# Wider modulation products through one row buffer, a softmax division and GpSimd's work on other engines, and a half-spectrum Fourier branch in both layers

## The chip, the cores and the metric

The kernel runs on one core of a Trainium2 chip. Its engines are TensorE (PE; its weight loads are PEld), VectorE (DVE), ScalarE (ACT), GpSimd (POOL), and SyncE (SP), which issues the DMAs; each runs its own instructions in order. The metric is the device time in microseconds of one execution.

## The reference

Two layers of a diffusion backbone, over 256 latent tokens (x) and 256 context tokens (ctx), 2048 channels wide. Both streams go through the same weights, each with its own modulation vector:

```python
mod = silu(c) @ ada_w[l] + ada_b[l]          # 3 x 2048: shift, scale, gate; once for c, once for c_ctx
h = rmsnorm(x, norm_g[l]) * (1 + scale) + shift
q, k, v, u_pool, u_four, g = split(h @ w_in[l])   # 1024, 256, 256, 512, 512, 2048
att  = attention(rope(norm(q)), rope(norm(k)), v)  # 8 heads, 2 kv heads; latents see context + latents
pool = multiscale_pool(u_pool, pool_w, pool_scale)
four = real(fft2(u_four per group of 128 channels, ortho)) @ fourier_w
x = x + gate * ((concat(att, pool, four) * silu(g)) @ w_out[l])
```

The second layer computes the latents alone past k and v, and the output is `rmsnorm(x, final_norm_g)` of the latents. The words "layer 1" and "layer 2" below mean the first and the second; in the code they are l = 0 and l = 1.

## The kernel before

**Matmuls.** All activations are held transposed (channels on the partitions), tokens as columns: 512 of them in layer 1, 256 of the latents in layer 2 past k and v. Each product of two fp32 matrices is made of three matmuls of fp32r halves (hi x hi, lo x hi, hi x lo; `mm3`, L331 to L333). A weight piece of 512 KB comes through `wpiece`: a DMA into `raw` (L146), ScalarE's cast to `whi` (L139), VectorE's subtraction to `wlo` (L140). Each of these three has 3 buffers. A piece is good for 24 matmuls 512 wide, or 48 narrower ones.

**The order of the work.** The program is written as one stream: in each layer the chunks of the input projection (pooling channels, Fourier channels, k and v, then two of q), with the branches' steps fed in between (`side`), then the gate tiles (`gate_evac`: tanh on ScalarE, `th`), the split of the gated mixed activations into `mh` and `ml`, and the output projection of 16 tiles (`finish`: `x` plus gate times the product at L676, its square `sq`, and the running sum of squares `accv`). A scheduler turns it once into a fixed list for each engine, by data dependences, buffers and priorities. Evacuations and weight pieces run at a higher priority (AHEAD), the modulation products at a low one (LOW).

**The modulation products.** Layer 1's shift and scale are made at the start by TensorE. The rest, gate of layer 1 and all of layer 2, is made by VectorE: 64 units of 128 rows of ada_w, transposed in `adar`, each times `cbt`, silu(c) and silu(c_ctx) on all partitions, with the sum over the row taken by the same instruction (`accum_out`, L189). Units below 48 need two products, for c and c_ctx, the last 16 one. A row of 2048 elements is done in two halves of 1024, in separate visits: 128 half units, 224 products. The buffers are

```python
cbt = rp.tile([P, 2, 1024], F32, tag="cbt", bufs=1, ...)
raw = rp.tile([P, 1024], F32, tag="araw", ...)          # rp has bufs=2
junk = rp.tile([P, 1024], BF16, tag="ajunk", bufs=1, ...)  # the products themselves, never read
```

`fill(n)` takes n steps of this generator after each weight piece (the fractions in FILL), and `fill_to` takes what is still due: 32 steps (16 units) ahead of layer 1's output projection, 96 at `between`, which stands in that projection's last tile and makes layer 2's scale and shift (`ab_98`, `ada_cols`) and its first `xn`, and 128 in layer 2. Each load waits by hand for the split of the weight piece that was last written (`pace`).

**The other places.** `rsqrt_small` (six calls, the q and k norms) starts on VectorE and runs three Newton steps of four operations on GpSimd. In the attention a head's probabilities `p` come from ScalarE's exp with their sum in `nm`, and VectorE multiplies by its reciprocal (L550); TensorE then transposes them (L562). `finish` adds the squares on GpSimd (L686, L688). The Fourier branch does two stages of matmuls: over the positions with a table (`dh`, `dl`), and over the channels with the folded tables `fh`, `fl`. Layer 1 uses the half table `dft0` (256 columns, cosines and sines of half of the spectrum) and restores the other half by a sum and a difference (`second0`); layer 2 uses the full one, `dft`, of 512 columns (`second1`).

The names `t2`, `f4`, `q8` are pools of general buffers: `t2` has 11 of 2 KB a partition, for `th`, `sq`, `p`, `xn`, `kraw` and the like.

## Time and profile before

| what | us |
| --- | --- |
| median of 3 runs | 1109.19 (1108.81 to 1110.93) |
| span of the profiled execution (its only time on the page) | 1107.6 |
| PE busy | 1066.2 |
| DVE busy | 849.3 |
| ACT busy | 451.7 |
| POOL busy | 83.0 |
| modulation products (L189), busy | 283.6 |

The span runs from the first to the last instruction of the profiled execution; the times of the runs hold what lies around it too. Busy shares are shares of the span. A group's row gives the line, the engine, the operation, output <- inputs, partitions x elements and the count; then busy time in us and the mean of one in ns; then the idle time of that engine just ahead of them, and what ended it. In the chain, a share is time in which the end of the program waited for this engine.

### The profile page before, as it was taken

The page shows a single profiled execution, that of the slowest core. Times are in us where ns is not written, and L with a number is a line of the kernel's source. Part 1 is how long each engine was busy: PE and PEld are TensorE (multiplying, and loading weights), DVE is VectorE, ACT ScalarE, POOL GpSimd, SP SyncE. Part 2 cuts the span into 40 slices and gives each one's busy share as a digit, 9 for nine tenths or more (in the row PEclk, how much of TensorE's full clock was granted, in tenths as well). Part 3 has the DMA queues.
Part 4 walks back from the last instruction along what each step waited for, and adds up shares of the span by engine and source line. Part 5 has one row for each costly group of instructions (what it writes and reads, how often), then busy time and mean ns, then how long its engine had stood idle before and what let it go on. Part 6 is the DMA issues. An engine that isn't in the chain of part 4 may idle for free.

```text
span 1107.6 us, 15377 instructions
## 1 busy us (share of the span) xinstructions
PE 1066.2 (96%) x5724; PEld 881.1 (80%) x5724; DVE 849.3 (77%) x1513; ACT 451.7 (41%) x741; POOL 83.0 (7%) x106
## 2 busy tenths in 40 slices
PE   5999999999899999999999999899999999999995
PEld 3566677888688888888888777788887899999995
DVE  6358647996968789999969998889646989767554
ACT  5223224323314554432522123288325656446552
POOL 0000000002003001000001111100002210001220
PEclk9899999999899999999999999999999999999998
DMA  9999667466653243566876777655665555765553
GB/s 358 406 334 336 226 230 242 158 192 198 214 185 118 73 143 124 153 205 232 283 249 220 225 220 257 208 170 177 239 192 171 166 190 170 260 206 187 184 180 94
DMA packets 66603, 231.89 MB, mean 209 GB/s; under 512 B 7200, under 2 KB 12384, under 8 KB 62944
## 3 DMA queue, kind: packets, MB, share of 16 engines
q1 hardware_dynamic: 66528, 230.91, 62.4%
q8 instruction: 45, 0.74, 0.3%
q14 instruction: 30, 0.25, 0.1%
HBM read 228.77 MB, written 2.11 MB: 208 GB/s over the span
## 4 chain that ended last, share of the span: by engine, by line
PE 74%; DVE 11%; DMA 8%; issue 4%; ACT 2%; POOL 1%; SPq 0%; DVEq 0%; ACTq 0%
PE mm L333 17%; PE mm L331 17%; PE mm L332 17%; PE mm L829 7%; DMA araw<-in_adar 5%; DVE ajunk L189 5%; PE sm L829 4%; DVE wlo L140 3%; PE sm L892 2%; PE sm L332 2%; PE sm L331 2%; PE sm L333 2%; PE sm L562 1%; DMA x<-in_xT 1%; ACT whi L139 1%
## 5 line engine op out<-in xcount | busy, mean ns | idle before, releaser
L140 DVE TENSOR_TENSOR wlo<-raw,whi 128x1024 fp32r<-128x1024 f32 (+1 forms) x216 | 256.1, 1186 | 125.0 <-ACT whi L139 124.4
L139 ACT CAST whi<-raw 128x1024 fp32r<-128x1024 f32 (+1 forms) x216 | 219.1, 1018 | 299.7 <-PE mm L332 134.3
L189 DVE SCALAR_TENSOR_TENSOR ajunk<-araw,cbt 128x1024 bf16<-128x1024 f32 x224 | 283.6, 1266 | 60.7 <-DMA araw<-in_adar 42.2
L333 PE MATMUL mm<-mh,wlo 128*128 128x256 f32 (+1 forms) x528 | 176.3, 334 | 6.2 <-DVE wlo L140 6.0
L331 PE MATMUL mm<-mh,whi 128*128 128x256 f32 (+1 forms) x528 | 175.1, 332 | 0.0
L332 PE MATMUL mm<-ml,whi 128*128 128x256 f32 (+1 forms) x528 | 174.8, 331 | 0.0
L331 PE MATMUL mm<-whi,hh 128*128 128x512 f32 x416 | 168.6, 405 | 4.5 <-DVE gpart L635 3.5
L332 PE MATMUL mm<-wlo,hh 128*128 128x512 f32 x416 | 164.3, 395 | 1.1 <-DVE wlo L140 1.1
L333 PE MATMUL mm<-whi,hl 128*128 128x512 f32 x416 | 164.0, 394 | 0.0
L331 PE MATMUL mm<-hh,whi 128*128 128x256 f32 (+1 forms) x452 | 151.0, 334 | 0.0
L332 PE MATMUL mm<-hl,whi 128*128 128x256 f32 (+1 forms) x452 | 149.1, 330 | 0.0
L333 PE MATMUL mm<-hh,wlo 128*128 128x256 f32 (+1 forms) x452 | 149.1, 330 | 0.0
L333 PEld LDWEIGHTS mm<-mh,wlo 128*128 128x128 f32 x528 | 100.2, 190 | 20.7 <-DVE wlo L140 11.6
L332 PEld LDWEIGHTS mm<-ml,whi 128*128 128x128 f32 x528 | 100.2, 190 | 9.7
L331 PEld LDWEIGHTS mm<-mh,whi 128*128 128x128 f32 x528 | 100.2, 190 | 9.3 <-ACT whi L139 0.4
L331 PEld LDWEIGHTS mm<-whi,hh 128*128 128x128 f32 x416 | 78.9, 190 | 21.9 <-DVE gpart L635 3.9
L332 PEld LDWEIGHTS mm<-wlo,hh 128*128 128x128 f32 x416 | 79.0, 190 | 17.6 <-DVE wlo L140 1.9
L333 PEld LDWEIGHTS mm<-whi,hl 128*128 128x128 f32 x416 | 78.8, 189 | 17.6 <-DVE hl L140 0.3
L333 PEld LDWEIGHTS mm<-hh,wlo 128*128 128x128 f32 x452 | 85.7, 190 | 8.2
L332 PEld LDWEIGHTS mm<-hl,whi 128*128 128x128 f32 x452 | 85.7, 190 | 7.9
L331 PEld LDWEIGHTS mm<-hh,whi 128*128 128x128 f32 x452 | 85.7, 190 | 7.6
L679 ACT ACTIVATE sq<-x 128x256 f32<-128x256 f32 (+1 forms) x33 | 16.9, 513 | 114.1 <-DVE x L676 114.1
(197 smaller groups left out, 1372.1 us busy)
## 6 DMA issues: line engine op xcount, KB each, us to landing
araw<-in_adar SPq DMA_DIRECT2D x128, 512.0 KB, 4.1
raw<-in_wb SPq DMA_DIRECT2D x78, 512.0 KB, 3.9
raw<-in_wo SPq DMA_DIRECT2D x64, 512.0 KB, 3.7
raw<-in_wg SPq DMA_DIRECT2D x55, 512.0 KB, 4.2
a<-in_ada SPq DMA_DIRECT2D x24, 1024.0 KB, 7.7
a<-in_ada SPq DMA_DIRECT2D x16, 512.0 KB, 5.0
x<-in_xT SPq DMA_DIRECT2D x4, 1024.0 KB, 7.2
cbt<-cd SPq DMA_DIRECT2D x7, 512.0 KB, 5.8
```

The source lines that it names most:

```text
L139: i = S.copy(hi, src)
L140: V.tensor_sub(lo, src, hi.bitcast(F32))
L189: V.scalar_tensor_tensor(junk, raw, 1.0, cbt[:, v], op0=ALU.mult, op1=ALU.mult, accum_out=acc[:, u, h, v : v + 1])
L331: PE.matmul(o, ah, bh, start=start, stop=False)
L332: PE.matmul(o, ah, bl, start=False, stop=False)
L333: PE.matmul(o, al, bh, start=False, stop=stop)
L562: PE.transpose(tp[:, h * P : h * P + P], ps[h][:, i * P : i * P + P], idt)
L679: S.activation(sq, x, AF.Square)
L829: PE.matmul(o, lt, r, start=s0, stop=s1)
L892: PE.matmul(a[32 * g : 32 * g + 32, :w_], cs[:, k], raw[:, i], start=kk == k_first, stop=kk == npc - 1, tile_position=(0, 32 * g))
```

## The change

Modulation products: a unit is one visit, 2048 wide, 112 products in all. `rp` has one buffer: one `cbt` of [128, 2, 2048] for the whole kernel, loaded once, and one `araw` of 2048, filled by two DMAs of 512 KB (L175). The first product of a unit below 48 writes its products as 8-bit floats into a tile of `t2` (L183, `ajunk`); a unit's last product writes them back into `araw` itself. A unit is still two steps of `fill`, the first of them after its first load. The sums of the two halves (`tensor_reduce`) are gone.

The softmax division goes from VectorE to ScalarE (L532). The additions of squares go from GpSimd to VectorE (L668); the first square is written into `accv` directly. A Newton step is three operations on VectorE instead of four on GpSimd. The Fourier branch uses `dft0` and `second` (the former `second0`, with `nst` streams) in both layers: layer 2's first stage has 24 matmuls of 256 columns instead of 512, the second 24 of 130 and 128 instead of 256. The `f4` pool has 4 buffers instead of 5.

```diff
-    late = {"f4": ctx.enter_context(tc.tile_pool(name="f4p", bufs=5))}
+    late = {"f4": ctx.enter_context(tc.tile_pool(name="f4p", bufs=4))}
...
-    acc = const.tile([P, 64, 2, 2], F32, name="acc")
+    acc = const.tile([P, 64, 2], F32, name="acc")
...
     def ada_units():
         rp = late["rp"]
-        cbt = None
-        segs = (
-            [(u, 0) for u in range(16)],
-            [(u, 1) for u in range(48)],
-            [(u, 0) for u in range(16, 64)],
-            [(u, 1) for u in range(48, 64)],
-        )
-        for seg in segs:
-            h = seg[0][1]
+        with tc.high_priority(offset=LOW):
+            cbt = rp.tile([P, 2, D], F32, tag="cbt", name="cbt")
+            for v in range(2):
+                nc.sync.dma_start(cbt[:, v], late["cd"][v].partition_broadcast(P))
+        for u in range(64):
             with tc.high_priority(offset=LOW):
-                cbt = rp.tile([P, 2, 1024], F32, tag="cbt", bufs=1, name=name("cbt"))
-                for v in range(2 if seg[0][0] < 48 else 1):
-                    nc.sync.dma_start(cbt[:, v], late["cd"][v, 1024 * h : 1024 * h + 1024].partition_broadcast(P))
-            for u, _ in seg:
-                with tc.high_priority(offset=LOW):
-                    raw = rp.tile([P, 1024], F32, tag="araw", name=name("araw"))
-                    d = nc.sync.dma_start(raw, adar[u, h])
+                raw = rp.tile([P, D], F32, tag="araw", name=name("araw"))
+                for h in range(2):
+                    c = slice(1024 * h, 1024 * h + 1024)
+                    d = nc.sync.dma_start(raw[:, c], adar[u, h])
                     tc.add_manual_dep(
                         d.ins, pace[0].ins.name, mybir.DependencyInfo(mybir.DependencyClass.Sync, mybir.DependencyReason.DATA)
                     )
-                    for v in range(2 if u < 48 else 1):
-                        junk = rp.tile([P, 1024], BF16, tag="ajunk", bufs=1, name=name("ajunk"))
-                        V.scalar_tensor_tensor(
-                            junk, raw, 1.0, cbt[:, v], op0=ALU.mult, op1=ALU.mult, accum_out=acc[:, u, h, v : v + 1]
-                        )
-                yield u
+                    if h == 0:
+                        yield u
+                for v in range(2 if u < 48 else 1):
+                    junk = t2("ajunk", (P, D), F8) if u < 48 and v == 0 else raw
+                    V.scalar_tensor_tensor(
+                        junk, raw, 1.0, cbt[:, v], op0=ALU.mult, op1=ALU.mult, accum_out=acc[:, u, v : v + 1], saturate=False
+                    )
+            yield u
...
     def ada_cols(dst, u0, b0):
         n = KT
-        V.tensor_reduce(dst, acc[:, u0 : u0 + n].rearrange("p u h v -> p u v h"), axis=AX.X, op=ALU.add)
-        V.tensor_add(dst, dst, adab[:, b0 : b0 + n].unsqueeze(2).to_broadcast([P, n, 2]))
+        V.tensor_add(dst, acc[:, u0 : u0 + n], adab[:, b0 : b0 + n].unsqueeze(2).to_broadcast([P, n, 2]))
...
-            G.tensor_mul(t, y, y)
-            G.tensor_mul(t, t, v)
-            G.tensor_scalar(t, t, -0.5 * f, 1.5 * f, op0=ALU.mult, op1=ALU.add)
-            G.tensor_mul(y, y, t)
+            V.scalar_tensor_tensor(t, y, -0.5 * f, y, op0=ALU.mult, op1=ALU.mult)
+            V.tensor_mul(t, t, v)
+            V.scalar_tensor_tensor(y, t, 1.5 * f, y, op0=ALU.add, op1=ALU.mult)
...
-        n = N if l == 0 else 512
-        dr = wp.tile([P, 2, n], F32, tag="raw", name=name("dft"))
-        nc.sync.dma_start(dr, dft0 if l == 0 else dft)
-        dh, dl = f4("dh", (P, 2, n)), f4("dl", (P, 2, n))
+        dr = wp.tile([P, 2, N], F32, tag="raw", name=name("dft"))
+        nc.sync.dma_start(dr, dft0)
+        dd = f4("dd", (P, 2, 2, N))
+        dh, dl = dd[:, 0], dd[:, 1]
...
-        def second1(g, z):
-            c = slice(g * P, g * P + P)
-            y = smt()
-            for i in range(2):
-                ci = slice(i * N, i * N + N)
-                mm3(y[:, :N], fh[:, i, c], fl[:, i, c], z[0][:, ci], z[1][:, ci], i == 0, i == 1)
-            S.copy(mixed[3][:, g, off : off + N], y[:, :N])
-
-        second = second0 if nst == 2 else second1
...
-                    mm3(z[:, s * n : s * n + n], u[0][:, 2 * s + mt, c], u[1][:, 2 * s + mt, c], dh[:, mt], dl[:, mt], mt == 0, mt == 1)
+                    mm3(z[:, s * N : s * N + N], u[0][:, 2 * s + mt, c], u[1][:, 2 * s + mt, c], dh[:, mt], dl[:, mt], mt == 0, mt == 1)
...
-            V.tensor_scalar(p[:, :nk], p[:, :nk], nm[:, 2, h : h + 1], None, op0=ALU.mult)
+            S.activation(p[:, :nk], p[:, :nk], AF.Copy, scale=nm[:, 2, h : h + 1])
...
-            sq = t2("sq", (P, nt))[:, n0:n1]
+            sq = accv[:, n0:n1] if k == 0 else t2("sq", (P, nt))[:, n0:n1]
...
-            if k == 0:
-                G.tensor_copy(accv[:, n0:n1], sq)
-            elif k < KT - 1:
-                G.tensor_add(accv[:, n0:n1], accv[:, n0:n1], sq)
-            else:
+            if 0 < k < KT - 1:
+                V.tensor_add(accv[:, n0:n1], accv[:, n0:n1], sq)
+            elif k:
...
-        late["rp"] = ctx.enter_context(tc.tile_pool(name="rp", bufs=2))
+        late["rp"] = ctx.enter_context(tc.tile_pool(name="rp", bufs=1))
```

How VectorE's order changes is shown at three places. In the rows, a name ends in a running number that tells tiles apart; `araw` is the row buffer, `ajunk` the junk tile, `acc` the column of sums.

*VectorE at the end of layer 1's chunk 2.* `vl` is the low half of v, taken out of TensorE's accumulators `mm`. Before:

```order
L189 SCALAR_TENSOR_TENSOR ajunk_2079,acc<-araw_2077,cbt_2074 128x1024 [waits DMAHW6_49,DMAHW0_49,DVE_49]
L189 SCALAR_TENSOR_TENSOR ajunk_2081,acc<-araw_2077,cbt_2074 128x1024 [waits DMAHW1_49,DVE_49]
L140 TENSOR_TENSOR wlo_2228<-raw_2225,whi_2227 128x1024 [waits DMAHW4_49,Activation_49]
L140 TENSOR_TENSOR vl_2122<-mm_1680,vh_2121 128x256 [waits PE_49,Activation_49]
L189 SCALAR_TENSOR_TENSOR ajunk_2115,acc<-araw_2113,cbt_2074 128x1024 [waits DMAHW3_49,DVE_49]
L140 TENSOR_TENSOR vl_2122<-mm_1681,vh_2121 128x256 [waits PE_49,Activation_49]
L189 SCALAR_TENSOR_TENSOR ajunk_2117,acc<-araw_2113,cbt_2074 128x1024 [waits DVE_49]
L140 TENSOR_TENSOR vl_2122<-mm_1682,vh_2121 128x256 [waits PE_49,Activation_49]
L189 SCALAR_TENSOR_TENSOR ajunk_2215,acc<-araw_2213,cbt_2074 128x1024 [waits DMAHW4_49,DVE_49]
L140 TENSOR_TENSOR vl_2122<-mm_1683,vh_2121 128x256 [waits PE_49,Activation_49]
L140 TENSOR_TENSOR wlo_2270<-raw_2267,whi_2269 128x512 [waits DMAHW7_49,Activation_49]
```

After (`mm_1661` to `mm_1664` are the same accumulators as `mm_1680` to `mm_1683` before):

```order
L183 SCALAR_TENSOR_TENSOR araw_1795,acc<-araw_1795,cbt 128x2048 [waits DVE_49]
L139 TENSOR_TENSOR wlo_2161<-raw_2158,whi_2160 128x1024 [waits DMAHW5_49,Activation_49]
L139 TENSOR_TENSOR wlo_2199<-raw_2196,whi_2198 128x512 [waits DMAHW6_49,Activation_49]
L183 SCALAR_TENSOR_TENSOR ajunk_1920,acc<-araw_1887,cbt 128x2048 [waits DMAHW5_49,DMAHW2_49]
L183 SCALAR_TENSOR_TENSOR araw_1887,acc<-araw_1887,cbt 128x2048 [waits DVE_49]
L183 SCALAR_TENSOR_TENSOR ajunk_1956,acc<-araw_1953,cbt 128x2048 [waits DMAHW7_49,DMAHW6_49]
L183 SCALAR_TENSOR_TENSOR araw_1953,acc<-araw_1953,cbt 128x2048 [waits DVE_49]
L183 SCALAR_TENSOR_TENSOR ajunk_2022,acc<-araw_1989,cbt 128x2048 [waits DMAHW1_49,DMAHW0_49]
L183 SCALAR_TENSOR_TENSOR araw_1989,acc<-araw_1989,cbt 128x2048 [waits DVE_49]
L183 SCALAR_TENSOR_TENSOR ajunk_2058,acc<-araw_2025,cbt 128x2048 [waits DMAHW3_49,DMAHW2_49]
L139 TENSOR_TENSOR vl_2064<-mm_1661,vh_2063 128x256 [waits Activation_49]
```

Between two splits earlier in this list, `wlo_1704`, the 32nd weight split in the order, and `vl_2064` there are now 17 products, 8.5 units, with nine splits between; the products that stood between the evacuations are now ahead of the first one.

*VectorE from the last gate tiles to the output projection.* `ml` is the low half of the gated mixed activations, `mix` times `th`. Before:

```order
L140 TENSOR_TENSOR wlo_4739<-raw_4736,whi_4738 128x1024 [waits DMAHW7_49,PE_49,Activation_49]
L733 SCALAR_TENSOR_TENSOR th_4577<-th_4577,mm_4498 128x512 [waits Activation_49]
L140 TENSOR_TENSOR ml_4602<-mix_1679,mh_4586 128x512
L600 SCALAR_TENSOR_TENSOR mix_1679<-mix_1679,th_4577 128x512 [waits DVE_49]
L140 TENSOR_TENSOR ml_4603<-mix_1679,mh_4587 128x512
L189 SCALAR_TENSOR_TENSOR ajunk_4567,acc<-araw_4565,cbt_2074 128x1024 [waits DMAHW0_49]
L140 TENSOR_TENSOR ml_4604<-mix_1679,mh_4588 128x512 [waits Activation_49]
L140 TENSOR_TENSOR wlo_4778<-raw_4775,whi_4777 128x1024 [waits DMAHW2_49,PE_49,Activation_49]
```

After:

```order
L183 SCALAR_TENSOR_TENSOR ajunk_4191,acc<-araw_4153,cbt 128x2048 [waits DMAHW6_49,DMAHW5_49]
L183 SCALAR_TENSOR_TENSOR araw_4153,acc<-araw_4153,cbt 128x2048 [waits DVE_49]
L183 SCALAR_TENSOR_TENSOR ajunk_4227,acc<-araw_4194,cbt 128x2048 [waits DMAHW7_49,DMAHW0_49]
L713 SCALAR_TENSOR_TENSOR th_4230<-th_4230,mm_4159 128x512 [waits Activation_49]
L183 SCALAR_TENSOR_TENSOR araw_4194,acc<-araw_4194,cbt 128x2048 [waits DVE_49]
L582 SCALAR_TENSOR_TENSOR mix_1660<-mix_1660,th_4230 128x512 [waits DVE_49]
L139 TENSOR_TENSOR ml_4403<-mix_1660,mh_4387 128x512 [waits Activation_49]
L183 SCALAR_TENSOR_TENSOR ajunk_4298,acc<-araw_4265,cbt 128x2048 [waits DMAHW2_49,DMAHW1_49]
L713 SCALAR_TENSOR_TENSOR th_4303<-th_4303,mm_4234 128x512 [waits Activation_49]
```

From `wlo_4461` to the last of the 16 `ml`, 45 rows, there are 7 units in the new order; a unit's two products now stand ahead of single `th`, `mix` and `ml` rows. From there to the last split of the output projection, `wlo_5596`, there are 11 units and 26 weight splits.

*VectorE at the layer boundary*, the last rows ahead of layer 2's first `xn`. Before:

```order
L213 TENSOR_REDUCE ab_98<-acc 128x32 [waits DVE_49]
L189 SCALAR_TENSOR_TENSOR ajunk_5817,acc<-araw_5815,cbt_4766 128x1024 [waits DMAHW5_49]
L140 TENSOR_TENSOR wlo_5866<-raw_5863,whi_5865 128x1024 [waits DMAHW1_49,PE_49,Activation_49]
L214 TENSOR_TENSOR ab_98<-ab_98,vt 128x32 [waits DVE_49]
L217 TENSOR_SCALAR ab_98<-ab_98 128x32 [waits DVE_49]
L218 TENSOR_TENSOR ab_98<-ab_98,vt 128x32 [waits DVE_49]
L189 SCALAR_TENSOR_TENSOR ajunk_5857,acc<-araw_5855,cbt_4766 128x1024 [waits DMAHW7_49]
L189 SCALAR_TENSOR_TENSOR ajunk_5861,acc<-araw_5859,cbt_4766 128x1024 [waits DMAHW0_49,DVE_49]
L676 SCALAR_TENSOR_TENSOR x_958_4647<-mm_5748,gate_99,x_958_4647 128x256 [waits PE_49]
L140 TENSOR_TENSOR wlo_5905<-raw_5902,whi_5904 128x1024 [waits DMAHW3_49,Activation_49]
```

After:

```order
L183 SCALAR_TENSOR_TENSOR ajunk_5403,acc<-araw_5400,cbt 128x2048 [waits DMAHW5_49,DMAHW4_49]
L668 TENSOR_TENSOR accv_4455<-accv_4455,sq_5440 128x512 [waits DVE_49,Activation_49]
L183 SCALAR_TENSOR_TENSOR araw_5400,acc<-araw_5400,cbt 128x2048 [waits DVE_49]
L183 SCALAR_TENSOR_TENSOR ajunk_5475,acc<-araw_5436,cbt 128x2048 [waits DMAHW7_49,DMAHW6_49]
L668 TENSOR_TENSOR accv_4455<-accv_4455,sq_5512 128x512 [waits DVE_49,Activation_49]
L183 SCALAR_TENSOR_TENSOR araw_5436,acc<-araw_5436,cbt 128x2048 [waits DVE_49]
L668 TENSOR_TENSOR accv_4455<-accv_4455,sq_5584 128x512 [waits DVE_49,Activation_49]
L207 TENSOR_TENSOR ab_98<-acc,vt 128x32 [waits DVE_49]
L210 TENSOR_SCALAR ab_98<-ab_98 128x32 [waits DVE_49]
L211 TENSOR_TENSOR ab_98<-ab_98,vt 128x32 [waits DVE_49]
L215 RECIPROCAL rstd_4456<-rstd_4456 128x256 [waits Activation_49]
L183 SCALAR_TENSOR_TENSOR araw_5508,acc<-araw_5508,cbt 128x2048 [waits DMAHW1_49,DMAHW0_49]
```

From `wlo_5596` to the first `xn` there are now 13 products: six units and the last product of a seventh, most of them behind the last work of the output projection.

*SyncE at the same place.* Before:

```order
L183 DMA araw_5737<-in_adar 128x1024 [waits DMAHW7_49,DMAHW2_49,DVE_49]
L146 DMA raw_5902<-in_wo 128x1024 [waits DMAHW3_49,DVE_49]
L183 DMA araw_5779<-in_adar 128x1024 [waits DMAHW4_49,DMAHW0_49,DVE_49]
L183 DMA araw_5815<-in_adar 128x1024 [waits DMAHW5_49,DMAHW2_49,DVE_49]
L146 DMA raw_5908<-in_wo 128x1024 [waits DMAHW6_49,DVE_49]
L183 DMA araw_5855<-in_adar 128x1024 [waits DMAHW4_49,DVE_49]
L183 DMA araw_5859<-in_adar 128x1024 [waits DMAHW5_49,DVE_49]
L146 DMA raw_6143<-in_wb 128x1024 [waits DMAHW1_49,DVE_49]
```

After:

```order
L175 DMA araw_5328<-in_adar 128x1024 [waits DMAHW2_49,DVE_49]
L175 DMA araw_5328<-in_adar 128x1024 [waits DMAHW3_49]
L175 DMA araw_5400<-in_adar 128x1024 [waits DMAHW3_49,DMAHW4_49,DMAHW2_49,DVE_49]
L175 DMA araw_5400<-in_adar 128x1024 [waits DMAHW5_49]
L175 DMA araw_5436<-in_adar 128x1024 [waits DMAHW5_49,DMAHW6_49,DMAHW4_49,DVE_49]
L175 DMA araw_5436<-in_adar 128x1024 [waits DMAHW7_49]
L175 DMA araw_5508<-in_adar 128x1024 [waits DMAHW6_49,DMAHW7_49,DMAHW0_49,DVE_49]
L175 DMA araw_5508<-in_adar 128x1024 [waits DMAHW1_49]
L175 DMA araw_5548<-in_adar 128x1024 [waits DMAHW1_49,DMAHW0_49,DVE_49]
L175 DMA araw_5548<-in_adar 128x1024
L145 DMA raw_5939<-in_wb 128x1024 [waits DVE_49]
```

Five units' loads, each pair behind the last product of the unit ahead of it, now stand in a row, and the first weights of layer 2 (`in_wb`) behind them.

More of the change, by code (lines that the diff above doesn't have):

```diff
@@ L15 @@
 I32 = mybir.dt.int32
-BF16 = mybir.dt.bfloat16
+F8 = mybir.dt.float8e4
 AF = mybir.ActivationFunctionType
@@ L73, in backbone @@
     icnt: bass.AP,
-    dft: bass.AP,
     dft0: bass.AP,
@@ L409, in fourier_branch, with second @@
         H2 = N // 2
-        def second0(g, z):
+        def second(g, z):
             c = slice(g * P, g * P + P)
-            zh, zl = (t.rearrange("p (s n) -> p s n", s=2) for t in z)
+            zh, zl = (t[:, :nt].rearrange("p (s n) -> p s n", s=nst) for t in z)
             y, w = smt(), smt()
-            yv = y[:, : 2 * H2 + 4].rearrange("p (s n) -> p s n", s=2)
-            wv = w[:, : 2 * H2].rearrange("p (s n) -> p s n", s=2)
+            yv = y[:, : nst * (H2 + 2)].rearrange("p (s n) -> p s n", s=nst)
+            wv = w[:, : nst * H2].rearrange("p (s n) -> p s n", s=nst)
             mm3(yv, fh[:, 0, c], fl[:, 0, c], zh[:, :, : H2 + 2], zl[:, :, : H2 + 2])
             mm3(wv, fh[:, 1, c], fl[:, 1, c], zh[:, :, H2:], zl[:, :, H2:])
-            ws = t2("w", (P, 2, H2))
+            ws = t2("w", (P, nst, H2))
             S.copy(ws, wv)
-            d = mixed[3][:, g].rearrange("p (s n) -> p s n", s=2)
+            d = mixed[3][:, g, off : off + nt].rearrange("p (s n) -> p s n", s=nst)
             S.copy(d[:, :, 0 : H2 + 1 : H2], yv[:, :, 0 : H2 + 1 : H2])
@@ L424, in second0 @@
             V.tensor_sub(d[:, :, H2 + 1 :], yv[:, :, 1:H2], ws[:, :, 1:])
-        def second1(g, z):
-            c = slice(g * P, g * P + P)
-            y = smt()
-            for i in range(2):
-                ci = slice(i * N, i * N + N)
-                mm3(y[:, :N], fh[:, i, c], fl[:, i, c], z[0][:, ci], z[1][:, ci], i == 0, i == 1)
-            S.copy(mixed[3][:, g, off : off + N], y[:, :N])
-        second = second0 if nst == 2 else second1
-        n = 512 // nst
         for g in range(4):
@@ L440, in fourier_branch @@
                 for mt in range(2):
-                    mm3(z[:, s * n : s * n + n], u[0][:, 2 * s + mt, c], u[1][:, 2 * s + mt, c], dh[:, mt], dl[:, mt], mt == 0, mt == 1)
+                    mm3(z[:, s * N : s * N + N], u[0][:, 2 * s + mt, c], u[1][:, 2 * s + mt, c], dh[:, mt], dl[:, mt], mt == 0, mt == 1)
             zh, zl = t2("zh", (P, 512), F32R), t2("zl", (P, 512), F32R)
-            split(z, zh, zl)
-            yield 1.28, 1.3
+            split(z[:, :nt], zh[:, :nt], zl[:, :nt])
+            yield 0.72 * nst, 1.3
             if prev:
                 second(*prev)
-                yield 0.64, 0.5
+                yield 0.36 * nst, 0.5
             prev = (g, (zh, zl))
@@ L999, in _tables @@
     sel[1::32, 1] = 1
-    return dict(rope=rope, band=band, icnt=icnt, dft=dft, dft0=dft0, cc=cc, sel=sel, ident=np.eye(P, dtype=f4))
+    return dict(rope=rope, band=band, icnt=icnt, dft0=dft0, cc=cc, sel=sel, ident=np.eye(P, dtype=f4))
 def _layout(x, c, ctx, c_ctx, ada_w, ada_b, norm_g, w_in, q_norm_g, k_norm_g, pool_w, pool_scale, fourier_w, w_out, final_norm_g):
@@ L1044, in _layout @@
     return {n: np.ascontiguousarray(a) for n, a in t.items()}
-_NAMES = ["xT", "vec", "cb", "ada0", "adar", "wb", "wg", "wo", "wgs", "gqk", "pw", "fw", "rope", "band", "icnt", "dft", "dft0", "cc", "sel", "ident"]
+_NAMES = ["xT", "vec", "cb", "ada0", "adar", "wb", "wg", "wo", "wgs", "gqk", "pw", "fw", "rope", "band", "icnt", "dft0", "cc", "sel", "ident"]
 def _result(y):
```

## The prediction

> **What bounds the kernel now.** I read first the busy shares and the shares of the chain of waits.
>
> ```profile
> PE 1066.2 (96%) x5724; PEld 881.1 (80%) x5724; DVE 849.3 (77%) x1513; ACT 451.7 (41%) x741; POOL 83.0 (7%) x106
> PE 74%; DVE 11%; DMA 8%; issue 4%; ACT 2%; POOL 1%; SPq 0%; DVEq 0%; ACTq 0%
> ```
>
> TensorE is busy for 96% of the span and carries 74% of the chain. So relieving VectorE (77%) is worth only what TensorE now waits for it, and a new wait ahead of TensorE costs its whole length. To see how much there is to win, I cut the span into five stretches (length; busy time of PE, PEld, DVE, ACT, POOL; granted clock; DMA share; GB/s).
>
> ```profile
> 205.00:260.00 55.00, 55.00 (x277) 46.89 (x276) 47.84 (x76) 15.88 (x28) 0.00 (x0) 1.00 0.62 201
> 260.00:300.00 40.00, 36.18 (x152) 28.98 (x152) 34.52 (x67) 14.76 (x31) 5.58 (x12) 0.93 0.59 192
> 300.00:530.00 230.00, 229.63 (x1087) 189.24 (x1087) 200.14 (x388) 91.12 (x161) 16.01 (x24) 1.00 0.49 156
> 530.00:730.00 200.00, 193.85 (x883) 157.72 (x881) 176.39 (x265) 62.17 (x86) 22.82 (x15) 1.00 0.71 232
> 730.00:1108.00 378.00, 362.46 (x2366) 329.25 (x2364) 264.06 (x439) 199.01 (x333) 38.39 (x51) 0.99 0.57 187
> ```
>
> Between 205 and 730 TensorE idles 0 + 3.8 + 0.4 + 6.2 = 10.4 us: that is all there is to win there. The idle part of 260 to 300 shows what a wait for VectorE does. The next rows are TensorE's timeline around it, the instruction of VectorE that ended it, and TensorE's windows (length, busy, clock).
>
> ```profile
> 291.40 0.39 PE L333 MATMUL mm<-whi,hl 128*128 128x512 f32 x1
> 295.25 0.80 PE L331 MATMUL mm<-whi,hh 128*128 128x512 f32 x1 [3.46 <-DVE gpart L635]
> 294.51 0.68 DVE L635 TENSOR_TENSOR gpart<-gpart,mm 128x512 f32<-128x512 f32 x1
> 290.00:294.00 4.00, 1.78 (x8) 1.00 0.66 226
> 294.00:298.00 4.00, 2.75 (x7) 0.57 0.58 170
> ```
>
> VectorE works in order; TensorE stood 3.46 us until gpart had its turn, and then got a clock of 0.57. So I look for places where the new order puts VectorE instructions that wait ahead of one that TensorE needs.
>
> **The modulation products.** Their rows: groups, DMA issues (KB, median us to landing), a wait of the DMA queue (total, times, longest), and the GB/s of the span's 40 slices.
>
> ```profile
> L189 DVE SCALAR_TENSOR_TENSOR ajunk<-araw,cbt 128x1024 bf16<-128x1024 f32 x224 | 283.6, 1266 | 60.7 <-DMA araw<-in_adar 42.2 <-DMA cbt<-cd 15.0
> L860 DVE SCALAR_TENSOR_TENSOR junk<-a,cq 128x512 f32<-128x512 f32 x16 | 10.5, 687 | 0.0
> araw<-in_adar SPq DMA_DIRECT2D x128, 512.0 KB, 4.1
> x<-in_xT SPq DMA_DIRECT2D x4, 1024.0 KB, 7.2
> SPq L183 <- DVE ajunk L189: 185.7, 86, 6.7
> GB/s 358 406 334 336 226 230 242 158 192 198 214 185 118 73 143 124 153 205 232 283 249 220 225 220 257 208 170 177 239 192 171 166 190 170 260 206 187 184 180 94
> ```
>
> The saving is small. 512 more elements cost 1266 - 687 = 579 ns, so a 2048-wide product takes 1266 + 2 x 579 = 2.42 us, and 112 of them save 112 x (2 x 1.266 - 2.42) = 12 us of VectorE. The price is the buffer. Before, two araw buffers alternate, so a load runs beside a product, and still the queue stood 185.7 us for a buffer. Now one buffer holds the unit, its last product writes into it, and the next load cannot be issued until that product is done: load and products add up. The load: 4.1 us for one transfer, and 512 KB more at the fastest slice's 406 GB/s are 1.3 us, so 5.4. Two products 4.85, issue 0.1: **10.3 us a unit**. Below, the pair takes no less than one transfer, 4.1 (9.1 a unit); above, as long as 1 MB of x in the crowded start, 7.2 (12.2). I take the value near the lower end, since in a row of units few other transfers run. Where VectorE has other work between units the load hides behind it; where units stand in a row it does not. By the Trainium skill ("Trainium Kernel Development and Optimization", Best Practices) one should double-buffer so that DMA overlaps compute; this change takes that away, and the 185.7 us show the queue short of buffers even with two. By that rule the change costs time; the sum below says how much.
>
> VectorE's new order has four such places. VectorE's own timeline gives when their ends are reached now:
>
> ```profile
> 205.76 1.22 DVE L140 TENSOR_TENSOR wlo<-raw,whi 128x1024 fp32r<-128x1024 f32 x1
> 259.32 0.42 DVE L140 TENSOR_TENSOR vl<-mm,vh 128x256 fp32r<-128x256 f32 x1
> 531.46 1.22 DVE L140 TENSOR_TENSOR wlo<-raw,whi 128x1024 fp32r<-128x1024 f32 x1
> 715.00 1.96 DVE L140 TENSOR_TENSOR wlo<-raw,whi 128x1024 fp32r<-128x1024 f32 x1 [0.28 <-ACT whi L139]
> 724.25 0.76 DVE L249 TENSOR_TENSOR xn<-x,rstd 128x256 f32<-128x256 f32 x2
> 157.71 5.44 PE mm L829 x24
> ```
>
> The last row, of the chain, is one weight piece: 24 matmuls in 5.44 us, 0.227 each.
>
> - **A, end of layer 1's chunk 2.** From the split that now runs at 205.76 to the first vl (259.32) stand 8.5 units: the first with its load already done (4.85), seven whole ones (72), the last with a load and one product (7.8), and some 7 us of other work: 92 us, until 298. TensorE's four accumulators wait for vl and kraw, and its next chunk for those. +38, less 6 that the present kernel loses in 260 to 300 anyway (3.8 idle and the slow clock): **+33** (+22 to +47).
> - **B, gates to first output tiles.** From the split at 531.46 to the last low half of the mixed activations stand 7 units and 12 us of other work: 7 x 10.3 + 12 = 84 us. TensorE has 186 matmuls to do meanwhile, 42 us, and the gate tiles queue behind the products too. **+42** (+34 to +55).
> - **C, the rest of the output projection.** 11 units, each with about 1.4 us of other work between its products (what stands behind its second product runs beside the next load): 11 x 11.7 = 129 us. TensorE has 23 weight pieces left there, 23 x 5.44 = 125, and the 6.2 idle of now. **-2** (-6 to +18 at 12.2 a unit).
> - **D, the layer boundary.** After the last split of the output projection (715.00 now) come six whole units and a load and a product of a seventh, ahead of the first xn of layer 2 (724.25 now). Nothing for TensorE stands between. 6 x 10.3 + 7.8 + 7 of other work = 77 against 9.25: **+68** (+59 to +81). SyncE has five units' loads there in a row, with layer 2's weights behind them.
> - **Clock.** Each such halt makes TensorE's restart slow: at 0.57 for 4 us about 2 us lost. Three halts, one of which is there now: **+4**. By the Trainium skill ("TensorE: Matmul & The Clock Gate", The HAM clock gate) an idle window of some 3.4 us drops the array to half clock for as long again; the 0.57 agrees, and by it the term would be at most 2 x 1.7 us.
>
> The single products of layer 2 (16 units, 7.8 us each) are spread over some 300 us there: 0 (0 to +5).
>
> **The other parts.**
>
> ```profile
> L550 DVE TENSOR_SCALAR p<-p,nm 128x512 f32<-128x512 f32 x32 | 15.4, 481 | 0.0
> L550 DVE TENSOR_SCALAR p<-p,nm 128x256 f32<-128x256 f32 x16 | 5.6, 350 | 0.1
> L545 ACT ACTIVATE p<-sm,nm,ny 128x512 f32<-128x512 f32 x32 | 24.8, 777 | 19.3 <-DVE nm L543 19.2
> L562 PE MATMUL sm<-idt,p 128*128 128x128 f32 x160 | 25.0, 273 | 0.4 <-ACT p L545 0.4
> L688 POOL TENSOR_TENSOR accv<-accv,sq 128x512 f32<-128x512 f32 x14 | 22.2, 1586 | 141.6 <-ACT sq L679 141.6
> L484 DVE TENSOR_TENSOR qo<-raw,tab 128x512 f32<-128x512 f32 x8 | 5.5, 688 | 0.0
> ACT qo L508 <- POOL ny L238: 16.4, 2, 10.5
> L331 PE MATMUL sm<-dh,q 128*128 128x512 f32 x8 | 3.1, 391 | 0.0
> L331 PE MATMUL sm<-zh,fh 128*128 128x256 f32 x6 | 1.7, 284 | 0.0
> ```
>
> *Softmax.* VectorE gives up 15.4 + 5.6 = 21 us; ScalarE, at 41%, takes at most 48 x 0.78 = 37. A head's chain grows by 0.78 - 0.48 = 0.3 us, but TensorE waits for p only 0.4 us in all, since other projection work covers it: 0 (were that cover gone, 48 x 0.3 = +14; were the 21 us of VectorE on the path, -21; the 0.4 puts it at 0). *Sums of squares.* 28 additions go to VectorE, at most 28 x 0.69 = 19 us. GpSimd waited 141.6 us for its operands, so it was not late; the additions stand among the units of C and D, where VectorE waits for loads: 0 (-2 to +5). *Newton steps.* ScalarE waited 16.4 us for them, 10.5 in A's stretch (counted in A); layer 2's remaining 6 are half on the path: **-3** (-6 to 0). *Fourier.* 24 first-stage matmuls go from 512 to 256 columns, 391 - 284 = 107 ns each: **-2.6**. The 24 of the second stage go from 256 to 130 or 128; the 128-wide ones above show 273 against 284, so 0 (0 to -3). The smaller table and one f4 buffer less: 0, for nothing waited on them here.
>
> **Sum.** 33 + 42 - 2 + 68 + 4 - 3 - 3 = +139. The span is 1107.6, the median of the three runs 1.6 above it: 1107.6 + 139 + 1.6 = **1248 us**. With 9.1 a unit everywhere it is 22 + 34 - 2 + 59 + 4 - 9 = +108 (1217), with 12.2 it is 47 + 55 + 18 + 81 + 4 - 3 = +202 (1311).
>
> **Rivals.**
> - *Faster.* VectorE has 12 + 21 us less to do, and every wait of TensorE on it between 205 and 730 vanishes: 10.4 + 2.6 gained, **1096**. It needs the rows of units to be no obstacle: at A a unit may take (53.5 - 7) / 8.5 = 5.5 us at most, which is 0.6 us beyond its products, so the loads would have to hide; at B and D even that does not do. Against it: one buffer, in order. The Trainium skill ("Perfetto Trace Analysis", Optimizing Scalar/DVE Operations) says that grouping work into larger operations improves throughput, but also that, on an engine not saturated, breaking instructions up may let work finish sooner. The first half is this rival; the rows give it 12 us of VectorE.
> - *Short loads.* Alone on the queues a pair lands in 4.1 us or less, and TensorE has more to do at A and B than I count, so only half of those two bites: 0.5 x (22 + 34) + 59 - 4 = +83, **1192**. For it: the slices up to 406 GB/s. Against: the median 4.1 was for half as much.
> - *Longer cycle.* At 12.2 a unit the output projection falls behind as well: **1311**, or some 1295 to 1315. For it: the 7.2 of the 1 MB transfers; against: those ran when everything was loading.
> - *No change* would need the units to lie in other places than the order says.
>
> **Chances.** Main case (1217 to 1290) 0.66; short loads 0.13; longer 0.14; faster 0.05; the same 0.02 (within 0.2%, about what a measurement of this kernel tells from no change). The range 1195 to 1295 holds the main case, half of the short-load case and a part of the longer one, some 0.8. Slower has 0.93.
>
> **What would show it.** TensorE idle some 33 us near 260 to 300, some 40 us before the output projection and over 60 us at the layer boundary, with VectorE's products there behind "DMA araw" and the queue's L175 behind "DVE araw"; GpSimd almost empty; the Fourier group at 128x256. I am wrong if a unit's cycle is near 5 us, if TensorE waits elsewhere, or if one of A, B, D shows no idle time.

## The result, and the profile after

The changed kernel takes 1266.94 us in the median (1261.63 to 1273.59, 4 runs) against 1110.06 us (1108.81 to 1113.65, 4 runs): a ratio of 1.1416, 95% interval 1.1386 to 1.1446. Forecast were 1248 us, 1195 to 1295. The profiled execution has a span of 1259.8 us, 152 more than before.

From the page of the changed kernel: busy time by engine, the chain of waits by engine, the groups of the products, two lines of the waits of all engines (engine, what it waited for: total, times, longest), and one of the DMA queue:

```profile
PE 1085.1 (86%) x5724; PEld 887.7 (70%) x5724; DVE 829.8 (66%) x1327; ACT 475.1 (38%) x793; POOL 0.2 (0%) x4
PE 51%; DVE 14%; DMA 11%; issue 4%; ACT 1%; SPq 1%; DVEq 0%; ACTq 0%
L183 DVE SCALAR_TENSOR_TENSOR ajunk<-araw,cbt 128x2048 fp8e4<-128x2048 f32 x48 | 109.9, 2290 | 131.7 <-DMA araw<-in_adar 125.9
L183 DVE SCALAR_TENSOR_TENSOR araw<-araw,cbt 128x2048 f32<-128x2048 f32 x64 | 146.3, 2285 | 20.5 <-DMA araw<-in_adar 20.1
PE sm L672 <- DVE accv L668: 46.4, 1, 46.4
PE mm L323 <- DVE vl L139: 39.0, 1, 39.0
SPq L175 <- DVE araw L183: 181.1, 48, 5.6
```

VectorE is busy 19.5 us less than before. TensorE's busy share of the span falls from 96% to 86%, and VectorE and DMA now make up a quarter of the chain. Two single halts alone, of 39.0 and 46.4 us, are more than half of the loss. The first, on VectorE's timeline (start, duration, and in brackets the idle time ahead and what ended it; the rows that only read out the sum are left out):

```profile
265.04 1.82 DVE L139 TENSOR_TENSOR wlo<-raw,whi 128x1024 fp32r<-128x1024 f32 x2 [1.21 <-ACT whi L138]
272.56 2.29 DVE L183 SCALAR_TENSOR_TENSOR ajunk<-araw,cbt 128x2048 fp8e4<-128x2048 f32 x1 [5.69 <-DMA araw<-in_adar]
274.89 2.29 DVE L183 SCALAR_TENSOR_TENSOR araw<-araw,cbt 128x2048 f32<-128x2048 f32 x1
282.21 2.29 DVE L183 SCALAR_TENSOR_TENSOR ajunk<-araw,cbt 128x2048 fp8e4<-128x2048 f32 x1 [5.02 <-DMA araw<-in_adar]
284.54 2.29 DVE L183 SCALAR_TENSOR_TENSOR araw<-araw,cbt 128x2048 f32<-128x2048 f32 x1
291.77 2.29 DVE L183 SCALAR_TENSOR_TENSOR ajunk<-araw,cbt 128x2048 fp8e4<-128x2048 f32 x1 [4.93 <-DMA araw<-in_adar]
294.11 2.29 DVE L183 SCALAR_TENSOR_TENSOR araw<-araw,cbt 128x2048 f32<-128x2048 f32 x1
301.44 2.29 DVE L183 SCALAR_TENSOR_TENSOR ajunk<-araw,cbt 128x2048 fp8e4<-128x2048 f32 x1 [5.04 <-DMA araw<-in_adar]
303.66 1.41 DVE L139 TENSOR_TENSOR vl<-mm,vh 128x256 fp32r<-128x256 f32 x4
```

This is a unit's cycle laid bare: wait for the load, two products, wait for the next load; 9.6 us from one unit to the next, half of it idle. The vl that TensorE needs is behind it in the queue. TensorE's first matmul afterwards, and its windows (length, busy, clock):

```profile
304.22 0.76 PE L323 MATMUL mm<-hh,whi 128*128 128x512 f32 x1 [38.99 <-DVE vl L139]
304.00:308.00 4.00, 3.78 (x10) 0.55 0.00 0
308.00:312.00 4.00, 4.00 (x19) 1.00 0.00 0
```

At the layer boundary VectorE goes through the same cycle, with an addition to accv (0.69 us) inside each unit:

```profile
840.39 2.29 DVE L183 SCALAR_TENSOR_TENSOR ajunk<-araw,cbt 128x2048 fp8e4<-128x2048 f32 x1 [3.42 <-DMA araw<-in_adar]
850.47 2.29 DVE L183 SCALAR_TENSOR_TENSOR ajunk<-araw,cbt 128x2048 fp8e4<-128x2048 f32 x1 [4.96 <-DMA araw<-in_adar]
860.54 2.29 DVE L183 SCALAR_TENSOR_TENSOR ajunk<-araw,cbt 128x2048 fp8e4<-128x2048 f32 x1 [4.96 <-DMA araw<-in_adar]
```

Ahead of the output projection the halt comes in pieces (total, times, longest):

```profile
PE mm L323 <- DVE th L713: 28.8, 5, 17.3
PE mm L323 <- ACT mh L138: 7.2, 1, 7.2
```

The table gives when VectorE starts certain instructions: splits of weight pieces, counted in the order of the list, and the first vl and xn. "Place alone" is what is lost from one of the prediction's places to the next; a slow clock after a halt is inside the measured numbers.

| VectorE starts | before | after | later by | prediction, place alone | measured, place alone |
| --- | --- | --- | --- | --- | --- |
| the 32nd weight split | 205.76 | 208.46 | 2.7 | | |
| the first vl (A) | 259.32 | 303.66 | 44.3 | | |
| the 52nd weight split (A over) | 323.46 | 362.02 | 38.6 | +33 | +38.6 |
| the 76th weight split | 504.29 | 554.11 | 49.8 | 0 | +11.2 |
| the 88th weight split (B over) | 573.59 | 669.25 | 95.7 | +42 | +45.9 |
| the 112th, last of the output projection (C) | 715.00 | 807.21 | 92.2 | -2 | -3.5 |
| the first xn of layer 2 (D) | 724.25 | 872.82 | 148.6 | +68 | +56.4 |
| end of the span | 1107.6 | 1259.8 | 152.2 | -6 | +3.6 |

### The profile page after: what moved, and what is told of

Read it like the earlier page. It is cut to its first block, busy times and chain, and to the rows that moved or that the text cites. A ratio compares the mean times of both kernels' runs of the same rounds, so it can differ in the third digit from the quotient of the medians.

```text
span 1259.8 us, 14978 instructions
## 1 busy us (share of the span) xinstructions
PE 1085.1 (86%) x5724; PEld 887.7 (70%) x5724; DVE 829.8 (66%) x1327; ACT 475.1 (38%) x793; POOL 0.2 (0%) x4
## 4 chain that ended last, share of the span: by engine, by line
PE 51%; DVE 14%; DMA 11%; issue 4%; ACT 1%; SPq 1%; DVEq 0%; ACTq 0%
PE mm L323 15%; PE mm L325 15%; PE mm L324 15%; DMA araw<-in_adar 11%; DVE araw L183 5%; DVE ajunk L183 3%; DVE wlo L139 3%; PE sm L323 2%; PE sm L324 2%; PE sm L325 2%; PE sm L544 1%; ACT whi L138 0%; SPq L175 0%; DVE accv L668 0%; PE sm L507 0%
## 5 line engine op out<-in xcount | busy, mean ns | idle before, releaser
L323 PE MATMUL mm<-mh,whi 128*128 128x256 f32 (+1 forms) x528 | 176.6, 339 | 25.5 <-DVE th L713 17.3
L183 DVE SCALAR_TENSOR_TENSOR ajunk<-araw,cbt 128x2048 fp8e4<-128x2048 f32 x48 | 109.9, 2290 | 131.7 <-DMA araw<-in_adar 125.9
L323 PE MATMUL mm<-whi,hh 128*128 128x512 f32 x416 | 165.3, 402 | 9.4 <-ACT hh L138 5.5
L183 DVE SCALAR_TENSOR_TENSOR araw<-araw,cbt 128x2048 f32<-128x2048 f32 x64 | 146.3, 2285 | 20.5 <-DMA araw<-in_adar 20.1
L325 PE MATMUL mm<-hh,wlo 128*128 128x256 f32 (+1 forms) x452 | 148.6, 334 | 0.0
L324 PEld LDWEIGHTS mm<-wlo,hh 128*128 128x128 f32 x416 | 78.6, 189 | 18.3 <-DVE wlo L139 2.4
```

Source lines behind the costliest of these rows:

```text
L183: V.scalar_tensor_tensor(junk, raw, 1.0, cbt[:, v], op0=ALU.mult, op1=ALU.mult, accum_out=acc[:, u, v : v + 1], saturate=False)
L323: PE.matmul(o, ah, bh, start=start, stop=False)
L324: PE.matmul(o, ah, bl, start=False, stop=False)
L325: PE.matmul(o, al, bh, start=False, stop=stop)
```

## The experiments

The theory: load and products in series through one buffer halt TensorE where units stand in a row. Rivals: the other parts of the change make the halts; the width does; or the place of the junk, for which the change uses t2, whose tiles come free in the order of the program.

**The other parts put back** (products and Fourier changed).

```diff
-            S.activation(p[:, :nk], p[:, :nk], AF.Copy, scale=nm[:, 2, h : h + 1])
+            V.tensor_scalar(p[:, :nk], p[:, :nk], nm[:, 2, h : h + 1], None, op0=ALU.mult)
...   (sums of squares and Newton steps on GpSimd, as before)
```

> The changed kernel with the softmax division, the sums of squares and the Newton steps put back as they were; the wide products through one buffer and the half-spectrum Fourier stay. VectorE's order has 8.5 units ahead of vl, 6 among the rows of ml and 5 ahead of the first xn (after: 8.5, 6, 6.5). Theory (load and products in series through one buffer, where units stand in a row): the three halts stay, of some 39, 42 and 50 us; 1240 to 1265 us. Rival (the work given to VectorE and ScalarE by the other parts makes the halts): near 1110 us.

Measured: 1269.09 us, ratio to before 1.1495 (1.1427 to 1.1564). The halts stay: TensorE waits 39.1 us at vl, in pieces of 18.3 us and less at the gates, and 18.8 and 25.4 us at the boundary. The wide products bring the whole loss; the half-spectrum Fourier branch, still in, is a small gain by itself (below).

**Narrow products, one buffer** (the kernel before, one edit).

```diff
-                    raw = rp.tile([P, 1024], F32, tag="araw", name=name("araw"))
+                    raw = rp.tile([P, 1024], F32, tag="araw", bufs=1, name=name("araw"))
```

> The kernel before, with one araw buffer of 1024 instead of two; nothing else. VectorE's order has 4 units ahead of vl, 0.2 among the rows of ml, and 13 units between the last split of the output projection and layer 2's first hl. Theory (load and products in series): a half unit takes 3.5 us of load, 2.5 of products and 0.2, a unit 12.4 us; the layer boundary halts TensorE for 13 x 12.4 - 9 = 150 us, the first two places next to nothing: 1240 to 1275 us, all of it at the boundary. Rival (the width of 2048 is what hurts): near 1115 us, for the products are as narrow as before.

Measured, one run: 1266.63 us. The waits of all engines show the boundary:

```profile
DVE ajunk L189 <- DMA araw<-in_adar: 219.9, 96, 4.8
PE mm L331 <- ACT hh L139: 143.2, 1, 143.2
```

One halt of 143.2 us, where 150 was expected (hh needs layer 2's scale and shift, and so the units). At the last split of the output projection, ahead of it, this kernel is only 3.4 us late. A second buffer is worth 157 us to the narrow products: the single buffer is enough for a loss of this size, and width is not needed for it.

**Two wide buffers** (the changed kernel).

```diff
-            cbt = rp.tile([P, 2, D], F32, tag="cbt", name="cbt")
+            cbt = rp.tile([P, 2, D], BF16, tag="cbt", name="cbt")
-                raw = rp.tile([P, D], F32, tag="araw", name=name("araw"))
+                raw = rp.tile([P, D], F32, tag="araw", bufs=2, name=name("araw"))
```

> The changed kernel with two araw buffers of 2048. Room for the second comes from cbt, which is held in bf16 (so silu(c) is rounded to bf16 in these products; nothing else is changed). VectorE's order is nearly that of the changed kernel at the first two places: 8.5 units ahead of vl, 6.5 among the rows of ml; ahead of the first xn half a unit instead of 6.5. Theory (the serial cycle of 9.6 us): a unit now takes its two products, 4.6 us, and the load hides; the first place needs 8.5 x 4.8 + 7 = 48 us where TensorE has 53, the second 6.5 x 4.8 + 12 = 43 against 42, so both halts go and the third with them: 1105 to 1125 us. Rival (the rows of units in the order, whatever the buffers, since a wide product cannot be passed): the halts at the first two places stay, 1180 us or more.

Measured: 1162.56 us, 1.0504 (1.0465 to 1.0544): 104 us better than with one buffer, but 53 above before, where at most 15 was expected. The halt at the boundary went; parts of A and B stayed. In its trace the first vl is 24.0 us late, the 76th split 26.3, the 88th 41.2, the first xn of layer 2 40.9 and the end 51.1. A product takes 2285 ns, so the bf16 cbt does not change its time. VectorE at A:

```profile
262.62 1.83 DVE L140 TENSOR_TENSOR wlo<-raw,whi 128x1024 fp32r<-128x1024 f32 x2 [3.68 <-ACT whi L139]
271.63 2.29 DVE L189 SCALAR_TENSOR_TENSOR ajunk<-araw,cbt 128x2048 fp8e4<-128x2048 f32 x1 [2.44 <-DMA araw<-in_adar]
276.19 2.29 DVE L189 SCALAR_TENSOR_TENSOR ajunk<-araw,cbt 128x2048 fp8e4<-128x2048 f32 x1
281.12 2.29 DVE L189 SCALAR_TENSOR_TENSOR ajunk<-araw,cbt 128x2048 fp8e4<-128x2048 f32 x1 [0.30 <-DMA araw<-in_adar]
283.34 1.41 DVE L140 TENSOR_TENSOR vl<-mm,vh 128x256 fp32r<-128x256 f32 x4
PE mm L329 <- DVE vl L140: 21.8, 2, 21.1
```

A unit now takes 4.6 to 4.9 us, as expected of the cycle. What was wrong is the count of the time: VectorE had waited earlier in the stretch, for ScalarE's casts of weights among others (3.68 us in the first row), so the last units were still to do when the accumulators were ready. The row itself costs 21 us here.

**A junk tile of its own** (the changed kernel, one araw buffer).

```diff
-T2 = 11
+T2 = 10
-                    junk = t2("ajunk", (P, D), F8) if u < 48 and v == 0 else raw
+                    junk = rp.tile([P, D], F8, tag="ajunk", bufs=1, name=name("ajunk")) if u < 48 and v == 0 else raw
```

> The changed kernel with a junk tile of its own for the first products instead of one from t2 (t2 has 10 buffers instead of 11 for the room, which by itself leaves the order as it is); one araw buffer still. VectorE's order now has 4 units ahead of vl and half a unit among the rows of ml, but 7 between the last split of the output projection and the first hl. Theory (one buffer is slow only where units stand in a row; the junk in t2 pulls units ahead of th and kraw, since t2's tiles come free in the order of the program): the first two halts go, the third stays with 7 x 9.7 - 9 = 59 us; 1155 to 1180 us. Rival (t2 has nothing to do with it, the one buffer alone sets the time): 1250 us or more. Rival (t2 alone does it, the buffer is harmless): near 1110 us.

Measured: 1197.79 us, 1.0823 (1.0781 to 1.0864), above the expected range, far from both rivals. The first vl is 2.2 us late instead of 44.3, and from the 76th to the 88th split nothing is lost; the boundary halts TensorE for 53.8 us:

```profile
PE mm L323 <- ACT hh L138: 53.8, 1, 53.8
```

Missed was a loss of 18.6 us between A and B (2.2 us late at vl, 20.8 at the 76th split), where 20 units share VectorE with the attention. So the rows of units at A and B came from t2's order, and the serial cycle made them long (with two buffers the same 8.5 units left vl 24.0 us late instead of 44.3): `ajunk` takes its turn among th, kraw and p, whose tiles cannot be had before the products ahead of them are done. The low priority cannot push a unit back past them.

**Both cures**: two wide buffers and a junk tile of its own.

> The changed kernel with both cures: two araw buffers of 2048 (cbt in bf16, so silu(c) is rounded in these products) and a junk tile of its own (t2 with 10 buffers). VectorE's order has 5 units ahead of vl, 1.5 among the rows of ml and none between the last split of the output projection and layer 2's first hl. Theory after the first four runs (two causes: load and products in series, and t2's order that pulls units together; each alone left 53 and 88 us): nothing is left of the loss, and the gain of the other parts shows, as with the narrow products (1090): 1085 to 1100 us. Rival (in SyncE's queue loads of 1 MB hold up the weights, as the first place still showed with two buffers): 1105 to 1130 us.

Measured: 1142.39 us, 1.0304 (1.0274 to 1.0333): neither the theory's 1085 to 1100 nor the rival's range. At the former places no halt over 4 us is left, but there are small ones all along. A group of this kernel and a wait of its DMA queue, and the same of the version with narrow products below:

```profile
L330 PE MATMUL sm<-ptl,vh 128*128 128x512 f32 x40 | 17.3, 433 | 5.9 <-DVE ptl L140 5.9
SPq L181 <- ACT whi L139: 194.6, 41, 20.9
```

```profile
L331 PE MATMUL sm<-ptl,vh 128*128 128x512 f32 x40 | 16.5, 412 | 1.1 <-DVE ptl L140 1.0
SPq L183 <- ACT whi L139: 74.8, 26, 9.0
```

TensorE waits five times as long for ptl, a small piece of the attention that shares VectorE with the wide products, and the queue waits longer for ScalarE's cast, the part of the split that paces its loads. These rows do not make up the 53 us between the two versions. By the two pages TensorE is idle 33 us longer, and its busy time is 19 us longer over the same 5724 matmuls. Nearly half of that idle time lies in layer 2, in waits of at most 3.8 us, for wlo, hh, th, ptl and pth. Which property of the wide products makes these waits (visits of 2.3 us, or loads of 1 MB among the weights' loads) no run here tells; it stays open.

**The narrow products with junk in t2** (the kernel before).

```diff
-                        junk = rp.tile([P, 1024], BF16, tag="ajunk", bufs=1, name=name("ajunk"))
+                        junk = t2("ajunk", (P, 1024), BF16)
```

> The kernel before with the junk of its 1024-wide products in tiles of t2 instead of a tile of its own; two buffers and all else as before. VectorE's order has 7.5 units ahead of vl (before: 5.8), 3 among the rows of ml (0.2) and 0.2 at the layer boundary. Theory (t2's order is a cause by itself): a part of the loss that two wide buffers still had, some 10 to 35 us at the first two places: 1115 to 1145 us. Rival (t2's order hurts only where load and products are in series): 1106 to 1112 us.

Measured: 1121.88 us, 1.0138 (1.0084 to 1.0191), as the theory has it: t2's order alone costs 14 us with narrow products and two buffers (20 with wide ones and two, 69 with wide ones and one). Its place is only in part the expected one: the first vl is 9.7 us late and TensorE waits 8.0 us for it, but 2.9 us of that are left at the 88th split. Most of the loss comes in the output projection: at its last split this kernel is 11.3 us late.

**The other parts without the products.** The changed kernel with `ada_units`, `ada_cols` and `rp` of before:

> The changed kernel with the modulation products of before (halves of 1024, two buffers): the softmax division, sums of squares, Newton steps and the half-spectrum Fourier alone. Theory (all of the loss is the products'): the prediction's -3 for the Newton steps, -2.6 for Fourier and some of the 6 us between 260 and 300: 1098 to 1107 us in the runs' median. Rival (the sums of squares and Newton steps load VectorE): 1112 us or more.

Measured: 1089.69 us, 0.9823 (0.9798 to 0.9849). It beats both kernels, and by more than expected. From its page:

```profile
PE 1057.2 (97%) x5724; PEld 878.2 (81%) x5724; DVE 839.6 (77%) x1555; ACT 475.0 (44%) x793; POOL 0.2 (0%) x4
```

The same parts one by one, each in the kernel before. The softmax division:

```diff
-            V.tensor_scalar(p[:, :nk], p[:, :nk], nm[:, 2, h : h + 1], None, op0=ALU.mult)
+            S.activation(p[:, :nk], p[:, :nk], AF.Copy, scale=nm[:, 2, h : h + 1])
```

> The kernel before with the softmax division on ScalarE alone. The prediction's term: 0, since TensorE waits for p 0.4 us in all; 1107 to 1112 us. Rival (a head's chain grows by 0.3 us and shows): +5 to +14. Rival (21 us less on VectorE show): -5 or more.

Measured: 1106.77 us, 0.9987 (0.9973 to 1.0001): 0, as forecast. Newton steps and sums of squares:

```diff
-            G.tensor_mul(t, y, y)
-            G.tensor_mul(t, t, v)
-            G.tensor_scalar(t, t, -0.5 * f, 1.5 * f, op0=ALU.mult, op1=ALU.add)
-            G.tensor_mul(y, y, t)
+            V.scalar_tensor_tensor(t, y, -0.5 * f, y, op0=ALU.mult, op1=ALU.mult)
+            V.tensor_mul(t, t, v)
+            V.scalar_tensor_tensor(y, t, 1.5 * f, y, op0=ALU.add, op1=ALU.mult)
...
-                G.tensor_add(accv[:, n0:n1], accv[:, n0:n1], sq)
+                V.tensor_add(accv[:, n0:n1], accv[:, n0:n1], sq)
```

> The kernel before with the Newton steps and the sums of squares on VectorE alone. The prediction's terms: -3 in layer 2 and some of the 6 us in 260 to 300, 0 for the sums of squares; 1100 to 1107 us. Rival (15 to 19 us more on VectorE, in the output projection, push other work): 1112 us or more.

Measured: 1097.1 us, 0.9901 (0.9876 to 0.9927): 10.7 us, the largest of the three. Part of what it does is seen in the modulation products, which this edit does not touch. Their row here, and one of them in the kernel before:

```profile
L189 DVE SCALAR_TENSOR_TENSOR ajunk<-araw,cbt 128x1024 bf16<-128x1024 f32 x224 | 273.5, 1221 | 63.2 <-DMA araw<-in_adar 47.9
702.17 2.19 DVE L189 SCALAR_TENSOR_TENSOR ajunk<-araw,cbt 128x1024 bf16<-128x1024 f32 x1
```

In the kernel before, nine of the 224 products take 2.1 to 2.3 us, and the others 1.21 to 1.24. The nine are the ones that start while GpSimd adds squares (L688; for the one shown, from 701.13 to 703.28). With GpSimd's work moved none takes over 1.23. So the additions on GpSimd cost VectorE 10 us in layer 1's output projection. How much of the 10.7 that is, and how much the shorter Newton chains are, no run here separates.

The half-spectrum branch:

```diff
-        dr = wp.tile([P, 2, n], F32, tag="raw", name=name("dft"))
-        nc.sync.dma_start(dr, dft0 if l == 0 else dft)
+        dr = wp.tile([P, 2, N], F32, tag="raw", name=name("dft"))
+        nc.sync.dma_start(dr, dft0)
...   (one `second` for both layers)
```

> The kernel before with the half-spectrum Fourier branch in layer 2 and four f4 buffers, alone. The prediction's term: -2.6 from the first stage, 0 to -3 from the second; 1104 to 1108 us. Rival (the sum and difference on VectorE and the smaller matmuls give it back): 1110 us.

Measured: 1105.06 us, 0.9966 (0.9947 to 0.9984): 2.8 us, the forecast term. Together the three make 14.6 us, the version with all of them gains 18.1.

**How many t2 buffers.** The last two use the narrow products with all other parts, and change `T2 = 11` to 10 and to 14.

> The version with the narrow products of before and all other parts of the change (1089.7), with 10 t2 buffers instead of 11. It tells what the remaining 53 us of the version with two wide buffers and its own junk tile come from, for that one had 10 as well. Theory (what is left there is the width: visits of 2.3 us and loads of 1 MB in front of other work): 1087 to 1095 us. Rival (the lost t2 buffer): 1105 us or more.

> The same version with 14 t2 buffers, for which the narrow products leave room. Theory (t2 is no limit for the narrow products): 1086 to 1093 us, as with 11. Rival (t2's tiles still hold up th, sq and p): faster by 5 us or more.

Measured: 1088.06 us (0.9822, 0.9799 to 0.9845) and 1087.91 us (0.9814, 0.9793 to 0.9834). The number of t2 buffers matters in neither direction, so the 53 us of the version with both cures are not the buffer that its t2 lacks, as far as the narrow products tell. This version, with 10, 11 or 14 alike, is the fastest of all that were run.

## Why the prediction was right, and where it was off

*The mechanism, right.* TensorE halts at A, B and D, with VectorE's products behind "DMA araw" and the queue's L175 behind "DVE araw", as listed under what would show it. The halts are 39.0 us at A and, in pieces, 36.6 between the 76th and the 88th split; at D it is 46.4 where over 60 was listed. The narrow products with one buffer show the cause by itself, and two buffers take 104 us off the changed kernel. The rule of the Trainium skill on double-buffering ("Trainium Kernel Development and Optimization", Best Practices) held: 157 us for the narrow products, 104 for the wide ones.

*The cycle.* Taken at 10.3 us (9.1 to 12.2), measured at 9.6 at the end of A and 10.1 in D. A product takes 2.29 us, not 2.42: the 1266 ns from which that was worked out are a mean that holds the nine long products. The products take 283.6 - 109.9 - 146.3 = 27.4 us less of VectorE and not 12, but 10.1 of these come from taking GpSimd's additions away (283.6 against 273.5) and 17.3 from the width. D came to +56 of the forecast +68: the first unit's load had already landed, and most of the other work counted there ran while a load was under way.

*A and B*, +33 and +42 in the sum, came to +38.6 and +45.9. For A, the 32nd split was already 2.7 us late, and from there to the first vl it took 95.2 us where 92 were counted. That this fits so well is in part luck: only the last units of the stretch stand 9.6 us apart; the five ahead of them, with splits and evacuations between, start 11.2 to 14.2 us apart, where the sum had 10.3 and 7 us of other work for the whole stretch. B's +45.9 holds some 10 us of slow clock, for which the sum had a term of its own. The prediction read the rows of units from the order and did not ask why they stood there: t2's order, which the run with a junk tile of its own shows. The edit that it passed over, the new place of the junk, is worth 69 us here.

*Between A and B* the sum had 0 and the trace +11.2; the run with its own junk tile loses 18.6 there. It is not a row: units start 9.7 to 49 us apart in the attention. TensorE is idle some 5 us longer than before, for ptl and other pieces of the attention, and where the rest goes stays open. *Layer 2* was to gain 6 us and lost 3.6. The version with narrow products gains 5.5 us there (it is 14.0 us earlier than before at the first xn and 19.5 at the end of the span), so the wide products cost some 9 us in layer 2, for which the sum had 0 (0 to 5).

*The other parts* were under-sized: -3 for Newton steps in layer 2, some of the 6 us in A, and 0 for the sums of squares, against 10.7 measured for both. The 0 rested on GpSimd not being late; that its additions hold up VectorE's products was not in the sum. Hardly any of the gain shows in the changed kernel: with these parts put back (and Fourier kept) it takes 1269.09 us, within the spread of the runs the same, and the two ratios' intervals (1.1386 to 1.1446, 1.1427 to 1.1564) overlap. A likely reason, not tested by itself, is that work saved on VectorE in a stretch is lost when the stretch ends in a wait for loads. Fourier (-2.6 against 2.8) and softmax (0 against 1.1, whose interval reaches 1) were right.

*The clock* (+4 for two more halts) was under-sized. The halt at A, 39 us long, is followed by 4 us at 0.55 and then by 1.00. Behind the one of 3.46 us before, the window after the last that the prediction shows, 298 to 302, still has 0.58, and only the next has 1.00. So what a halt costs in clock does not grow with it, but a restart can take more than the 4 us counted, and at B each of several pieces has its own. By the trace's clock records TensorE works 42 us at 0.5 in the changed kernel and 15 before; half of the difference, some 13 us, is an estimate of the term. By the Trainium skill ("TensorE: Matmul & The Clock Gate", The HAM clock gate) full speed is back after at least one busy window of about 3.4 us, as long as the idle window that took it; the rows at A agree with one such window, the 6.8 us at 0.5 before with two.

*The rivals.* "Faster" needed a unit to fit into 5.5 us at A; it took 9.6. "Short loads" was nearest in its premise, for a pair of loads leaves VectorE idle 4.9 to 5.0 us between products, less than the 5.5 of load and issue taken, but A and B bit in full. "Longer cycle" needed 12.2 us a unit and got 9.6 to 10.1 in the rows; C, where it was to bite, lost nothing.
